# Expert stage of a hybrid layer: four couples of experts instead of two take their tokens straight from memory, empty slots are left out, and the sorted rows are fetched and transposed among the first couples' products

## The chip, the cores and the metric

The program runs on one core of a Trainium2 chip. A core has TensorE (PE) for matrix products, VectorE (DVE), ScalarE (ACT) and GpSimd (POOL) for elementwise work, SyncE (SP), from which the kernel's ordinary DMAs are issued, and 16 DMA engines that move data between memory (DRAM) and the core's SBUF. Products land in PSUM, eight banks of 128x512 float32. The metric is the device time of one execution in microseconds, as the median of three runs.

## The reference

Two layers over 512 tokens of width 1024: the first has attention, pooling and a gated MLP, the second neighbourhood attention, a gated delta rule and a hierarchical mixture of experts. The change lies in the mixture alone:

```python
N_EXPERTS, TOP_K_IN_GROUP, D_EXPERT = 64, 2, 256
def hierarchical_moe(h, wg_r, bg_r, we_r, be_r, w_gate, w_up, w_down):
    ...  # group by argmax, two experts in the group by top_k, softmax gates
    def expert_block(args):
        tok, e = args
        xb = h_pad[tok]
        hid = jax.nn.silu(xb @ w_gate[e]) * (xb @ w_up[e])
        return hid @ w_down[e]
    ...  # each row times its gate, added to its token
...
x = x + hierarchical_moe(rms_norm(x, ln2_g), ...)
```

All 64 experts' weights are read, 3 MB of float32 each; 1024 rows (512 tokens, two experts each) go through them.

## The kernel before

**Slots and couples.** Each expert has 64 slots (`CAP`). Experts e and e + 32 make a couple, whose 128 slots are the 128 rows of one tile; the 32 couples are run in order (`pr_`). A loop for experts with more than 64 rows follows, which these inputs never enter.

**One couple.** `gate_up` multiplies the transposed tokens `xw` (128 features x 8 x 128 slots) by the gate and up weights `wgu` of both experts into one bank, `pgu`, 32 products; ScalarE makes `sg` and VectorE `hid` from it. `turn` transposes `hid` into `phT`, which ScalarE evicts. `down` multiplies by `wd` into two banks, `pd`, and both halves are scaled by the gates and split into a coarse and a fine part, `og` (ScalarE, then VectorE). `combine` multiplies `og` by `OT`, which has a one where a slot belongs to a token, and so adds the rows to their tokens: the left 512 columns (n = 0) into four banks kept over all couples, `pkept`; the right 512 (n = 1) into passing banks, `pcmb`, which VectorE adds to `xn`. The order of TensorE's instructions is that of the code (a manual schedule): gate-up of couple p, down of p - 1, turn of p, combine of p - 1. The other engines' orders are set by the scheduler.

**Banks.** The eight banks go by tags, each tag's in turn: `banks = dict(mm=2, pa=2, pb=2, pc=1, gv=1)`. `pa` holds `pgu` and `phT`, `pb` holds `pd` and `pcmb`; from the first combine on `mm`, `gv` and `pc` are the four `pkept`.

**Weights.** For each couple SP issues four transfers `wgu` (10 buffers) and two `wd` (4 buffers) in one queue, each when the buffer before it is free.

**Tokens.** `xn`, the layer's input to the experts, is written to DRAM as `xs`. Couples 0 and 1 take their tokens directly: `first_i` holds each slot's token (0 for an empty slot), an indirect DMA from GpSimd's queue fetches 128 rows into `xg`, and `gather` transposes them in eight 128x128 pieces into two `pb` banks (`pxg`), each evicted by one VectorE instruction that multiplies by the norm's gain. For all later couples the 1024 rows are sorted by expert: `ptok` and vector work ahead of it give `tok_of`, `compact` fetches and transposes eight blocks of 128 sorted rows into `xgT`, and `window` copies the 64 columns of each expert from there into `xw` on GpSimd. Blocks 0 to 3 stand behind gate-up 0 and blocks 4 to 7 behind gate-up 1:

```python
                hid = gate_up(pr_)
                if first and pr_ < 2:
                    compact(4 * pr_, 4 * pr_ + 4)
```

`pgt` is the table of gates by slot (`gt`).

Of the kernel before, what the change touches and what calls it, by code (L numbers as in the profile page):

```python
# [19 lines left out]
S = 512  # L20
# [69 lines left out]
def hybrid_kernel(ctx, tc, A, out, dbg=None):  # L90
# [1205 lines left out]
    xn = [lp.tile([128, D], F32, name=f"xn{t}") for t in range(4)]  # L1296
    NPAIR = 32
# [52 lines left out]
    for c in range(4):  # L1350
        hi, lo = split_w(A["wout2"][c])
        cs = slice(c * 256, c * 256 + 256)
        for t in range(4):
# [6 lines left out]
            nc.vector.scalar_tensor_tensor(xn[t][:, cs], p[:, 256:512], ra[:, t:t + 1],  # L1360
                                           xin[2 * t + c // 2][:, c % 2 * 256:c % 2 * 256 + 256], op0=ALU.mult, op1=ALU.add)
            nc.vector.tensor_tensor(xn[t][:, cs], xn[t][:, cs], p[:, 0:256], op=ALU.add)
            nc.scalar.activation(jk, xn[t][:, cs], AF.Square, accum_out=sq3[:, t, c:c + 1])
            if c % 2:
                nc.sync.dma_start(xs[ts, c * 256 - 256:c * 256 + 256], xn[t][:, c * 256 - 256:c * 256 + 256])
# [19 lines left out]
        for k in (2 * c, 2 * c + 1):  # L1385
            pt = ps("pb", "xnT")
            for t in range(4):
                nc.tensor.transpose(pt[:, t * 128:t * 128 + 128], xn[t][:, k * 128:k * 128 + 128], ident)
# [98 lines left out]
    def gather(tok, dst, xg):  # L1487

        nc.gpsimd.indirect_dma_start(out=xg, out_offset=None, in_=xs,
                                     in_offset=bass.IndirectOffsetOnAxis(ap=tok, axis=0))  # L1490
        for q in range(2):
            p = ps("pb", "pxg")
            for j in range(4):
                nc.tensor.transpose(p[:, j * 128:j * 128 + 128], xg[:, (4 * q + j) * 128:(4 * q + j) * 128 + 128], ident)
            nc.vector.tensor_tensor(dst[:, 4 * q:4 * q + 4, :], p.rearrange("p (j s) -> p j s", j=4),
                                    V("ln2", 4 * q, 4).unsqueeze(2).to_broadcast([128, 4, 128]), op=ALU.mult)


    t2, t2r = mt("t2", (128, 8, 2)), mt("t2r", (128, 8, 2), F32R)
    one_hot(t2, e31)  # L1500
    nc.vector.tensor_tensor(t2r, t2, pay[:, :, :, 0].rearrange("p t k -> p (t k)").unsqueeze(2).to_broadcast([128, 8, 2]),
                            op=ALU.mult)
    ohs = slots("a")
    pf = ps("pc", "pfirst")
    for i in range(8):
        nc.tensor.matmul(pf[:, 0:2], ohs[:, i, :], t2r[:, i, :], start=(i == 0), stop=(i == 7))
    first_i = mt("first_i", (128, 2), I32)
    nc.vector.tensor_copy(first_i, pf[:, 0:2])
    first = []

    def direct(i):
        first.append(et("xw", (128, 8, 128)))
        gather(first_i[:, i:i + 1], first[i], et("xg", (128, D)))

    direct(0)
    direct(1)


    few = et("few", (128, 256), tag="hid")
    ge, tokb, cend = cut(few, 0, 4, 2, 9), cut(few, 72, 4, 2, 8), cut(few, 136, 64)  # L1520
    tokr, cnt, cst_ = mt("tokr", (128, 4, 2, 8), F32R), mt("cnt", (128, 64)), mt("cst_", (128, 64))
    nc.vector.tensor_copy(cnt, pk[:, 0:64])
    nc.vector.tensor_tensor_scan(cend, cnt, iota[:, 0:1].to_broadcast([128, 64]), 0.0, op0=ALU.add, op1=ALU.add)
    nc.vector.tensor_tensor(cst_, cend, cnt, op=ALU.subtract)
    place, base = m4("place", 2), m4("base", 2)
    nc.vector.tensor_tensor(scr, M, cst_.unsqueeze(1).to_broadcast([128, 8, 64]), op=ALU.mult)
    nc.vector.tensor_reduce(base, scr, axis=AX.X, op=ALU.add)
    nc.vector.tensor_tensor(place, base, rank, op=ALU.add)

    nb, sp = m4("nb", 2), m4("sp", 2)  # L1530
    nc.vector.tensor_tensor(ge, place.unsqueeze(3).to_broadcast([128, 4, 2, 9]),
                            edges.unsqueeze(1).unsqueeze(1).to_broadcast([128, 4, 2, 9]), op=ALU.is_gt)
    nc.vector.tensor_reduce(nb, ge[:, :, :, 1:8], axis=AX.X, op=ALU.add)
    nc.vector.scalar_tensor_tensor(sp, nb, -128.0, place, op0=ALU.mult, op1=ALU.add)
    nc.vector.tensor_tensor(tokb, ge[:, :, :, 0:8], ge[:, :, :, 1:9], op=ALU.subtract)
    nc.vector.tensor_tensor(tokr, tokb, pay[:, :, :, 0:1].to_broadcast([128, 4, 2, 8]), op=ALU.mult)
    pi = ps("pc", "ptok")
    for i in range(2):
        o = et("ohp", (128, 4, 128), F32R, tag="OT")
        one_hot(o, sp[:, 2 * i:2 * i + 2, :])  # L1540
        for j in range(4 * i, 4 * i + 4):
            nc.tensor.matmul(pi[:, 0:8], o[:, j % 4, :], tokr[:, j // 2, j % 2, :], start=(j == 0), stop=(j == 7))
    tok_of = mt("tok_of", (128, 8), I32)
    nc.vector.tensor_copy(tok_of, pi[:, 0:8])
# [37 lines left out]
    def compact(b0, b1):  # L1582
        for b in range(b0, b1):
            gather(tok_of[:, b:b + 1], xgT[:, :, b * 128:b * 128 + 128],
                   et("xg", (128, D)) if b // 2 % 2 else big("xg"))
# [6 lines left out]
    def moe_round(pre, wts, gt, first=()):  # L1592
# [58 lines left out]
        def combine(OT, ab, start=False, stop=False):  # L1651
# [3 lines left out]
            for n, t in ((0, 0), (0, 1), (1, 0), (0, 2), (1, 1), (0, 3), (1, 2), (1, 3)):  # L1655
# [13 lines left out]
        with tc.manual_schedule(engines={mybir.EngineType.PE}):  # L1669
            prev = None  # L1670
            for pr_ in range(NPAIR):
# [4 lines left out]
                if first and pr_ < 2:  # L1676
                    compact(4 * pr_, 4 * pr_ + 4)
# [122 lines left out]
```

## Time and profile before

| | us |
|---|---|
| median of three runs | 1586.71 (1580.32 to 1591.32) |
| the profiled execution's own time | 1585.05 |
| its span on the core | 1583.3 |
| TensorE busy in the span | 1484.3 (94%) |
| VectorE, ScalarE, GpSimd busy | 843.9, 503.3, 247.0 |

The rows of the trace come from the profiled execution, so a sum over them stands against 1585.05 and its span of 1583.3. A stretch such as 1065:1070 counts microseconds from the span's start; the expert stage begins near 1050 and ends with the span. PEclk is the TensorE clock that was granted, 1.00 for 2.4 GHz and 0.50 for 1.2 GHz. A busy share is a mean over stages that differ, so the stage is read by itself.

### The profile page before, as it was taken

How to read it: one execution, taken by the hardware profiler on the slowest of the kernel's cores; microseconds unless marked ns; L12 is line 12 of the kernel's file. 1: busy time of each engine (PE TensorE's matmuls, PEld its weight loads, DVE VectorE, ACT ScalarE, POOL GpSimd, SP SyncE). 2: the span in 40 equal slices, each digit the busy share in tenths (PEclk: the TensorE clock that was granted, in tenths of full speed). 3: DMA queues.
4: the chain of work that ended last, by engine and by line, in shares of the span. 5: the costliest groups of instructions: out<-in, count | busy, mean ns of one | idle time of the engine just before them, and what ended most of it. 6: DMA issues, size and time to landing. Idle time of an engine off the chain costs nothing.

```text
span 1583.3 us, 20312 instructions
## 1 busy us (share of the span) xinstructions
PE 1484.3 (94%) x7485; PEld 1006.7 (64%) x7485; DVE 843.9 (53%) x1673; ACT 503.3 (32%) x933; POOL 247.0 (16%) x314
## 2 busy tenths in 40 slices
PE   6989999999999999998879999968999999999997
PEld 2756686888888887876667787964444434444443
DVE  3669777563564457275796666554323323333334
ACT  3444434441342345263434435320111111111111
POOL 0233011000000005224551330101100000000000
PEclk8979999999999999998989999988999999999999
DMA  8664242322233223363332123658899999999983
GB/s 302 225 212 130 68 146 89 111 94 93 95 103 96 93 80 101 98 190 95 86 103 64 44 81 101 240 224 333 325 412 421 421 420 420 420 421 421 420 363 109
DMA packets 81741, 327.22 MB, mean 207 GB/s; under 512 B 17624, under 2 KB 21336, under 8 KB 57312
## 3 DMA queue, kind: packets, MB, share of 16 engines
q1 hardware_dynamic: 80192, 320.58, 54.6%
q0 software_dynamic: 1440, 5.24, 1.0%
q8 instruction: 61, 1.00, 0.3%
q14 instruction: 48, 0.39, 0.1%
HBM read 317.32 MB, written 8.47 MB: 206 GB/s over the span
## 4 chain that ended last, share of the span: by engine, by line
PE 71%; DVE 11%; DMA 6%; ACT 4%; POOL 3%; issue 3%; SPq 1%; POOLq 0%; ACTq 0%; DVEq 0%
PE pgu L1612 13%; PE pj L177 10%; PE pj L179 10%; PE pj L178 10%; PE pd L1641 7%; PE pcmb L1660 2%; DVE wlo L171 2%; DMA graw<-in_modw_dram 2%; PE pcmb L1659 2%; DVE og L198 2%; DMA xg<-xs,tok_of 1%; ACT og L194 1%; DVE cv L872 1%; PE pS L482 1%; PE pkept L1659 1%
## 5 line engine op out<-in xcount | busy, mean ns | idle before, releaser
L177 PE MATMUL pj<-hh,whi 128*128 128x512 f32 x640 | 260.0, 407 | 19.3 <-ACT cn L866 8.1
L179 PE MATMUL pj<-hh,wlo 128*128 128x512 f32 x640 | 257.4, 403 | 2.4 <-DVE wlo L171 2.4
L178 PE MATMUL pj<-hl,whi 128*128 128x512 f32 x640 | 257.9, 403 | 0.6 <-DVE hl L200 0.6
L1612 PE MATMUL pgu<-wgu,xw 128*64 128x512 f32 x1024 | 226.8, 595 | 0.0
L171 DVE TENSOR_TENSOR wlo<-wraw,whi 128x1024 fp32r<-128x1024 f32 (+4 forms) x126 | 151.5, 1205 | 51.0 <-ACT whi L170 47.9
L170 ACT ACTIVATE whi<-wraw 128x1024 fp32r<-128x1024 f32 (+4 forms) x126 | 129.1, 1027 | 136.9 <-PE pj L178 116.6
L1612 PEld LDWEIGHTS pgu<-wgu,xw 128*64 128x64 f32 x1024 | 70.7, 137 | 139.2 <-issue 138.8
L177 PEld LDWEIGHTS pj<-hh,whi 128*128 128x128 f32 x640 | 124.0, 194 | 53.7 <-ACT cn L866 10.6
L179 PEld LDWEIGHTS pj<-hh,wlo 128*128 128x128 f32 x640 | 124.1, 194 | 32.7 <-issue 4.4
L178 PEld LDWEIGHTS pj<-hl,whi 128*128 128x128 f32 x640 | 123.7, 193 | 28.0 <-issue 2.1
L1618 DVE SCALAR_TENSOR_TENSOR hid<-pgu,agt,sg 128x256 f32<-128x256 f32 x32 | 15.5, 483 | 200.8 <-ACT sg L1616 200.8
L1616 ACT ACTIVATE sg<-pgu,agt 128x256 f32<-128x256 f32 x32 | 15.2, 475 | 330.2 <-PE pgu L1612 330.2
L1641 PE MATMUL pd<-wd,hT 128*64 128x512 f32 x512 | 116.0, 595 | 0.2 <-issue 0.2
L1663 DVE TENSOR_TENSOR xn<-xn,pcmb 128x512 f32<-128x512 f32 x128 | 85.1, 685 | 33.7 <-PE pcmb L1660 33.7
L1603 POOL COPY xw<-xgT 128x512 f32 x60 | 35.1, 614 | 404.5 <-PE pgu L1612 386.2
L304 POOL TENSOR_TENSOR acc<-acc,sq 128x512 f32<-128x512 f32 x21 | 33.7, 1623 | 392.8 <-ACT sq L303 392.6
L198 DVE SCALAR_TENSOR_TENSOR og<-pd,agt,og 128x512 fp32r<-128x512 f32 x64 | 48.0, 750 | 78.3 <-ACT og L194 78.3
L1641 PEld LDWEIGHTS pd<-wd,hT 128*64 128x64 f32 x512 | 37.1, 138 | 73.1 <-issue 64.5
L194 ACT ACTIVATE og<-pd,agt 128x512 fp32r<-128x512 f32 x64 | 44.0, 688 | 89.5 <-PE pd L1641 89.5
L179 PE MATMUL pj<-ah,wlo 128*128 128x512 f32 x176 | 69.3, 394 | 0.0
L177 PE MATMUL pj<-ah,whi 128*128 128x512 f32 x176 | 69.3, 394 | 0.0
L178 PE MATMUL pj<-al,whi 128*128 128x512 f32 x176 | 69.3, 394 | 0.0
(445 smaller groups left out, 2602.9 us busy)
## 6 DMA issues: line engine op xcount, KB each, us to landing
wgu<-in_egu_dram SPq DMA_DIRECT2D x128, 1024.0 KB
wd<-in_ed_dram SPq DMA_DIRECT2D x62, 1024.0 KB
graw<-in_modw_dram SPq DMA_DIRECT2D x48, 512.0 KB
wraw<-in_wup_dram SPq DMA_DIRECT2D x42, 512.0 KB
wraw<-in_win_dram SPq DMA_DIRECT2D x38, 512.0 KB
wraw<-in_wdn_dram SPq DMA_DIRECT2D x20, 512.0 KB
wraw<-in_wout_dram SPq DMA_DIRECT2D x16, 512.0 KB
E<-gscr SPq DMA_DIRECT2D x16, 256.0 KB
```

Source lines behind the costliest of these rows:

```text
L170: nc.scalar.activation(hi, raw, AF.Copy)
L171: nc.vector.tensor_tensor(lo, raw, hi.bitcast(F32), op=ALU.subtract)
L177: nc.tensor.matmul(p, whi, hh, start=first, stop=False)
L178: nc.tensor.matmul(p, whi, hl, start=False, stop=False)
L179: nc.tensor.matmul(p, wlo, hh, start=False, stop=last)
L194: nc.scalar.activation(hi, src, AF.Identity, scale=scale, bias=0.0 if bias is None else bias)
L198: nc.vector.scalar_tensor_tensor(lo, src, scale, hi.bitcast(F32), op0=ALU.mult, op1=ALU.subtract)
L1603: nc.gpsimd.tensor_copy(xw[:, :, 64 * i:64 * i + 64], xgT[:, :, bass.ds(r, 64)])
L1612: nc.tensor.matmul(gu[64 * i:64 * i + 64, :], xw[:, j, 64 * i:64 * i + 64], wts.gu[e][j], start=(j == 0), stop=(j == 7))
L1641: nc.tensor.matmul(pd[64 * i:64 * i + 64, :], hT[:, j, 64 * i:64 * i + 64], wts.d[e][:, j, n * 512:n * 512 + 512], start=(j == 0), stop=(j ...
L1659: nc.tensor.matmul(pc, OT[:, ts], a, start=(n == 1 or start), stop=False, skip_group_check=(n == 0))
L1663: nc.vector.tensor_tensor(v, v, pc, op=ALU.add)
```

## The change

Four couples (`NFIRST`) take their tokens directly. An empty slot's index is now 1024, beyond the bound of 511, so that its row is not fetched; the two `xg` buffers are set to zero ahead (GpSimd). The list of the sorted rows (`sorted_tokens`, with `ptok`) stands behind gate-up 0, and so do the transposes of couples 2 and 3. The eight sorted blocks are transposed behind gate-up 1 (0, 1), combine 0 (2), gate-up 2 (3, 4), combine 1 (5) and gate-up 3 (6, 7), in `pa` and `pb`; block b + 2 is fetched when block b has been transposed. Of each pair of evictions one stays on VectorE, the other is four 128x128 instructions on ScalarE. `xn` is split: its left halves, `xl`, give their buffers to the `xw` of couples 2 and 3 and are loaded again from `xs` for the last combine; the right halves are `xr`. In `combine` the third `pkept` comes before the first `pcmb`, and the third `pcmb` uses `pa`. In the code after, `raw` are the rows fetched for the first couples, and `between` is called at the places named.

```diff
+    xl = [lp.tile([128, 2, S], F32, tag="xl", name="xl", bufs=2) for i in range(2)]
+    xr = [lp.tile([128, S], F32, name=f"xr{t}") for t in range(4)]
+    xn = [(xl[t // 2][:, t % 2, :], xr[t]) for t in range(4)]
+    NPAIR, NFIRST = 32, 4
...
-    def gather(tok, dst, xg):
+    def fetch(tok, xg, **kw):
 
         nc.gpsimd.indirect_dma_start(out=xg, out_offset=None, in_=xs,
-                                     in_offset=bass.IndirectOffsetOnAxis(ap=tok, axis=0))
+                                     in_offset=bass.IndirectOffsetOnAxis(ap=tok, axis=0), **kw)
+        return xg
+
+    def features(xg, dst, tags=("pb", "pb")):
+
         for q in range(2):
-            p = ps("pb", "pxg")
+            p = ps(tags[q], "pxg")
             for j in range(4):
                 nc.tensor.transpose(p[:, j * 128:j * 128 + 128], xg[:, (4 * q + j) * 128:(4 * q + j) * 128 + 128], ident)
-            nc.vector.tensor_tensor(dst[:, 4 * q:4 * q + 4, :], p.rearrange("p (j s) -> p j s", j=4),
-                                    V("ln2", 4 * q, 4).unsqueeze(2).to_broadcast([128, 4, 128]), op=ALU.mult)
...
+            if q == 0:
+                nc.vector.tensor_tensor(dst[:, 0:4, :], p.rearrange("p (j s) -> p j s", j=4),
+                                        V("ln2", 0, 4).unsqueeze(2).to_broadcast([128, 4, 128]), op=ALU.mult)
+            else:
+                for j in range(4):
+                    nc.scalar.activation(dst[:, 4 + j, :], p[:, j * 128:j * 128 + 128], AF.Copy, scale=V("ln2", 4 + j))
...
+    def fetch_first(i):
+        xg = et("xg", (128, D))
+        if i < 2:
+            nc.gpsimd.memset(xg, 0.0)
+        return fetch(first_i[:, i:i + 1], xg, bounds_check=S - 1, oob_is_err=False)
...
+    def fetch_block(b):
+        blocks[b] = fetch(tok_of[:, b:b + 1], big("xg") if b < 2 else et("xg", (128, D)))
+
+    def block_features(b):
+        features(blocks[b], xgT[:, :, b * 128:b * 128 + 128], ("pa", "pb") if b % 2 == 0 else ("pb", "pa"))
+        if 2 <= b + 2 < 8 and b >= 2:
+            fetch_block(b + 2)
...
+        if at == "start":
+            features(raw[0], first[0])
+            raw.append(fetch_first(2))
+            features(raw[1], first[1])
+            raw.append(fetch_first(3))
+        elif at == ("up", 0):
+            sorted_tokens()
+            fetch_block(0)
+            fetch_block(1)
+            for i in (2, 3):
+                first.append(new_first(i))
+                features(raw[i], first[i], ("pa", "pb"))
+                fetch_block(i)
+        elif at == "last":
+
+            for i in range(2):
+                xl[i] = lt("xl", (128, 2, S), tag="xl", bufs=2)
+                nc.sync.dma_start(xl[i], xs[256 * i:256 * i + 256, 0:S].rearrange("(t p) c -> p t c", t=2))
...
+        for b in {("up", 1): (0, 1), ("add", 0): (2,), ("up", 2): (3, 4), ("add", 1): (5,), ("up", 3): (6, 7)}.get(at, ()):
+            block_features(b)
...
-            for n, t in ((0, 0), (0, 1), (1, 0), (0, 2), (1, 1), (0, 3), (1, 2), (1, 3)):
+            for n, t in ((0, 0), (0, 1), (0, 2), (1, 0), (0, 3), (1, 1), (1, 2), (1, 3)):
                 a, b = ab[n]
                 ts = slice(t * 128, t * 128 + 128)
-                pc = ps("pb", "pcmb") if n else kept[t]
+                pc = ps("pa" if t == 2 else "pb", "pcmb") if n else kept[t]
```

On TensorE, between the last product of gate-up 0 and the first of gate-up 1, there stood before (four blocks of the sorted rows, then the turn of couple 0):

```order
L1612 MATMUL pgu_9309<-wgu_8744,xw_9191 64x512
L1494 MATMUL pxg_9332<-cst_64,xg_9330 128x128 x4
L1494 MATMUL pxg_9338<-cst_64,xg_9330 128x128 x4
...
L1494 MATMUL pxg_9374<-cst_64,xg_9372 128x128 x4
L1494 MATMUL pxg_9380<-cst_64,xg_9372 128x128 x4
L1626 MATMUL phT_9386<-cst_64,hid_9328 128x128 x2
L1612 MATMUL pgu_9405<-wgu_9076,xw_9206 64x512
```

and stands now:

```order
L1662 MATMUL pgu_9317<-wgu_8746,xw_9261 64x512
L1592 MATMUL ptok_9338<-tokr_9242,ohp_9339 128x8 x4
L1592 MATMUL ptok_9338<-tokr_9242,ohp_9345 128x8 x4
L1501 MATMUL pxg_9357<-cst_64,xg_9286 128x128 x4
L1501 MATMUL pxg_9363<-cst_64,xg_9286 128x128 x4
L1501 MATMUL pxg_9375<-cst_64,xg_9305 128x128 x4
L1501 MATMUL pxg_9381<-cst_64,xg_9305 128x128 x4
L1676 MATMUL phT_9392<-cst_64,hid_9336 128x128 x2
L1662 MATMUL pgu_9411<-wgu_9078,xw_9262 64x512
```

The four sorted blocks have left this place; `ptok` and the transposes of couples 2 and 3 have come.

On TensorE, in the combine of couple 0 behind the turn of couple 1, there stood before (`pkept_9505` to `_9508` are the four kept banks):

```order
L1659 MATMUL pkept_9506<-og_9487,OT_9391 128x512
L1660 MATMUL pkept_9506<-og_9487,OT_9391 128x512
L1659 MATMUL pcmb_9513<-og_9495,OT_9391 128x512
L1660 MATMUL pcmb_9513<-og_9495,OT_9391 128x512
L1659 MATMUL pkept_9507<-og_9487,OT_9391 128x512
L1660 MATMUL pkept_9507<-og_9487,OT_9391 128x512
```

and stands now (`pkept_9485` to `_9488`):

```order
L1709 MATMUL pkept_9486<-og_9467,OT_9397 128x512
L1710 MATMUL pkept_9486<-og_9467,OT_9397 128x512
L1709 MATMUL pkept_9487<-og_9467,OT_9397 128x512
L1710 MATMUL pkept_9487<-og_9467,OT_9397 128x512
L1709 MATMUL pcmb_9495<-og_9475,OT_9397 128x512
L1710 MATMUL pcmb_9495<-og_9475,OT_9397 128x512
L1709 MATMUL pkept_9488<-og_9467,OT_9397 128x512
```

A third kept pair has come ahead of the first passing one, in every couple.

On GpSimd, whose queue holds the gathers, there stood before (the last six of ten gathers are left out):

```order
L1416 MEMSET xgT_9093 128x8x64
L1489 DMA xg_9192<-xs_8464,first_i_9189 128x1024
L1489 DMA xg_9207<-xs_8464,first_i_9189 128x1024
L1489 DMA xg_9358<-xs_8464,tok_of_9253 128x1024
L1489 DMA xg_9372<-xs_8464,tok_of_9253 128x1024
```

and stand now:

```order
L1524 MEMSET xg_9193 128x1024
L1524 MEMSET xg_9198 128x1024
L1492 DMA xg_9193<-xs_8466,first_i_9191 128x1024
L1492 DMA xg_9198<-xs_8466,first_i_9191 128x1024
L1492 DMA xg_9286<-xs_8466,first_i_9191 128x1024
L1492 DMA xg_9305<-xs_8466,first_i_9191 128x1024
L1492 DMA xg_9352<-xs_8466,tok_of_9260 128x1024
```

Two memsets have come ahead, and there are twelve gathers instead of ten.

## Rows read from the trace of the kernel before

**Rows 1.** Table by stretches: each engine's busy us, PEclk, DMA share, GB/s.

```profile
core 0: us, PE busy (x) PEld busy (x) DVE busy (x) ACT busy (x) POOL busy (x), PEclk, DMA share, GB/s
1065.00:1070.00 5.00, 1.87 (x8) 1.78 (x8) 4.05 (x19) 0.00 (x0) 2.16 (x2) 0.50 0.49 146
1100.00:1105.00 5.00, 1.84 (x8) 1.47 (x8) 1.59 (x3) 0.00 (x0) 0.00 (x0) 0.71 1.02 423
1120.00:1125.00 5.00, 5.00 (x26) 1.68 (x24) 0.48 (x1) 0.48 (x1) 1.17 (x2) 1.00 0.76 269
1125.00:1130.00 5.00, 4.95 (x23) 2.66 (x20) 2.19 (x3) 1.65 (x3) 0.00 (x0) 1.00 1.02 428
1200.00:1300.00 100.00, 99.60 (x442) 42.46 (x440) 34.80 (x55) 14.39 (x27) 7.03 (x12) 1.00 1.01 420
```

**Rows 2.** Chain of work that ended last: start us, us, what.

```profile
1065.14 5.54 DMA xg<-xs,first_i
...
1089.32 16.31 DMA xg<-xs,tok_of
...
1146.53 7.02 PE pgu L1612 x32
1153.55 3.48 PE pd L1641 x16
...
1551.51 7.02 PE pgu L1612 x32
```

**Rows 3.** Order of time ahead of gate-up 0: start, us, instruction, [idle before it <-releaser].

```profile
1065.14 1.21 POOL L1489 DMA_INDIRECT xg<-xs,first_i  x1 [11.38 <-DVE first_i L1508]
...
1067.58 1.87 PE L1542 MATMUL ptok<-tokr,ohp 128*128 128x8 f32 x8 [2.94 <-DVE ohp L1470]
...
1070.72 1.97 PE L1494 MATMUL pxg<-cst,xg 128*128 128x128 f32 x8 [1.27 <-DMA xg<-xs,first_i]
...
1074.13 1.38 PE L1494 MATMUL pxg<-cst,xg 128*128 128x128 f32 x8
...
1076.31 1.94 PE L1612 MATMUL pgu<-wgu,xw 128*64 128x512 f32 x8
```

**Rows 4.** The tile `xg`: the gathers' time from issue to landing.

```profile
DMA to landing us min/median/max: 4.3/5.9/16.3
```

**Rows 5.** Groups of instructions by form: count, busy us, mean ns, idle before.

```profile
L1495 DVE TENSOR_TENSOR xgT<-pxg,vec 128x512 f32<-128x512 f32 x16 | 10.5, 685 | 12.6 <-PE pxg L1494 12.6
...
L510 ACT ACTIVATE PT<-pT 128x128 f32<-128x128 f32 x32 | 8.0, 270 | 10.7 <-DVE PT L512 10.7
```

**Rows 6.** Order of time: two gathers issued, and the transposes behind their landing.

```profile
1086.30 0.94 POOL L1489 DMA_INDIRECT xg<-xs,tok_of  x1 [0.66 <-PE pxg L1494]
...
1087.88 0.94 POOL L1489 DMA_INDIRECT xg<-xs,tok_of  x1 [0.65 <-PE pxg L1494]
...
1098.26 1.06 PE L1494 MATMUL pxg<-cst,xg 128*128 128x128 f32 x8 [0.95 <-DMA xg<-xs,tok_of]
1102.01 1.84 PE L1494 MATMUL pxg<-cst,xg 128*128 128x128 f32 x8 [2.69 <-DMA xg<-xs,tok_of]
```

**Rows 7.** Order of time on TensorE, part of a combine (couple 1).

```profile
1128.15 0.40 PE L1659 MATMUL pcmb<-og,OT 128*128 128x512 f32 x1
1128.59 0.50 PE L1660 MATMUL pcmb<-og,OT 128*128 128x512 f32 x1
1128.93 0.39 PE L1659 MATMUL pkept<-og,OT 128*128 128x512 f32 x1
1129.16 0.40 PE L1660 MATMUL pkept<-og,OT 128*128 128x512 f32 x1
...
1130.80 0.50 PE L1659 MATMUL pcmb<-og,OT 128*128 128x512 f32 x1
1131.14 0.39 PE L1660 MATMUL pcmb<-og,OT 128*128 128x512 f32 x1
```

**Rows 8.** The page's DMA issues: count, KB each.

```profile
wgu<-in_egu_dram SPq DMA_DIRECT2D x128, 1024.0 KB
```

**Rows 9.** Two of SP's issues of weights beside couple 2, in order of time.

```profile
1120.15 4.24 SPq L1311 DMA_DIRECT2D wgu<-in_egu_dram  x4
1127.02 0.80 SPq L1321 DMA_DIRECT2D wd<-in_ed_dram  x2
```

## What the change should do to the time

> **What bounds the kernel.** I read the table by stretches first, then the chain of waits, the order of time around the change, and the DMA views. From the expert stage on TensorE is busy 99.6% of the time with the clock granted in full, while the weights stream at 420 GB/s and the 16 DMA engines are busy throughout [rows 1]. Which of the two sets the pace? The chain of waits has no weight transfer in it: it runs through TensorE, and each couple of experts takes the same time, (1551.51 - 1146.53) / 27 = 15.00 us [rows 2]. So TensorE's own order is the bound there, with the weights close behind. Ahead of it lies a stretch of waiting: the first couple's gather is 5.54 us of the chain, a later one 16.31 us, TensorE is busy 1.84 us in the five from 1100, and the granted clock falls to 0.50 (1.2 GHz) from 1065 and to 0.71 in the mean at 1100 [rows 1, 2]. The first gate-up product starts at 1076.31 [rows 3]; the fifth (couple 4) at 1146.53, 70.2 us later [rows 2]. The change touches the start, these 70.2 us, and one thing in every later couple: the order of the adds.
>
> **The start.** Up to the first gather nothing on the path changes: `first_i` is computed for four couples instead of two in instructions of a few columns. The two memsets stand ahead of it on GpSimd, which was idle for 11.38 us there [rows 3], so they cost nothing; if that cover were gone they would delay the gather by their own length, two instructions of 128x1024. The first gather is issued at 1065.14 and takes 5.54 us [rows 2] for 128 rows, of which those of the empty slots are all token 0. An expert has on average 512 x 2 / 64 = 16 tokens for 64 slots, so about a quarter of the rows is left. No row shows a gather of a quarter. The quickest whole one takes 4.3 us [rows 4]; the bounds are 5.5 (nothing gained) and, since some data must still come, 3.3; I take 4.3, because that is a measured gather without repeated rows. Landing: 1069.4. The Trainium skill (DMA: Bandwidth & Descriptors, "Anatomy of one DMA - SWDGE (gpsimd) path") gives about 2.0 us and the bytes at 436 GB/s, which is 3.2 us for 128 rows, where the trace has 4.3 at best, and 2.3 us for a quarter; by it the start would come 2.0 us earlier than I take and the sum below would be 1567.
>
> The sorted rows' list, 1.87 us of `ptok` at half clock and the vector work behind it, leaves this stretch, and the gate table `pgt` moves into the wait for the gather, where it is hidden. After landing: eight transposes of couple 0, 1.97 us in the order of time before; couple 1's second bank then waits until ScalarE has emptied couple 0's second one in four pieces. A 128x128 eviction on ScalarE is 270 ns [rows 5], so 1.1 us against 0.69 us for VectorE's one instruction; then four transposes at half clock, 0.9 us (half of the 1.97, or 1.38 for eight across a clock change [rows 3]). 1069.4 + 2.0 + 1.1 + 0.9 = 1073.4 instead of 1076.31: **2.9 us** gained, 1.6 with the slow landing, 3.9 with the quick one.
>
> **Couples 0 to 3.** TensorE's work from the first gate-up to that of couple 4, at the new pace of a couple (14.57 us, next part): three whole couples 43.7, gate-up and turn of the fourth 7.4, the 64 transposes of the sorted rows 8 x 1.06 = 8.5 [rows 6], those of couples 2 and 3 2.1, `ptok` 0.9 at full clock. Sum 62.6. New is one wait for a bank: `pa` has two, and couple 3's first transposes need the one that gate-up 0 fills, so they wait for `sg` and `hid` behind it, some 1.3 us with the vector work queued ahead; 63.9. Then the gathers. Four in a row beside the weights landed 3.75 us apart (1098.26, 1102.01), and the second had been issued 11.96 us before [rows 6], so a single one takes about 11.96 - 3.75 + 1.6 (their distance at issue) = 9.8 us. Now they are issued far ahead: blocks 0 and 1 about 8.5 us after the first gate-up starts, needed at 18.6; block 4 is issued when block 2 is transposed, at 30, and needed at 38. That is 1 to 2 us late in two or three places. I take 3 us, between 0 and 6. 63.9 + 3 = 66.9 against 70.2: **3.3 us** gained, between 0.3 and 6.3. ScalarE gets eight half blocks of 1.1 us in a stretch where it is nearly idle, and the evictions of `pd` stand behind two of them; TensorE needs longer for the transposes and `pd` itself than ScalarE for these, so I cost that at nothing. If that cover fails, a couple costs 1 us more.
>
> **Every couple: the order of the adds.** Matmuls of this part normally start 0.23 us apart (1128.93 to 1129.16). The one at 1128.59 starts 0.44 us after its forerunner, waiting for VectorE's second half of `og`, and the restart costs 0.34 instead of 0.23 to the next; at 1130.80 the last `pcmb` waits for a bank that VectorE has to empty, and its restart is 0.34 again [rows 7]. Excess: 0.21 + 0.11 + 0.11 = 0.43 us in 15.00. Now a third `pkept` pair stands ahead, 0.47 us, which is more than the 0.21 of waiting; and the third `pcmb` goes to `pa`, so the last one needs a bank that was read one add earlier. `pa` is free then: its other users, the gate-up and `phT`, have been read. So 15.00 becomes 14.57. Late next would be the weights. Couples 4 to 31 give 27 x 0.43 = 11.6, the last combine in the loop 0.4: **12.0 us**. The tail behind it (eight adds on VectorE and the outputs) keeps its length; the reload of `xl` is 1 MB (2.5 us at 420 GB/s) in the middle of the weights' queue.
>
> **Do the weights keep up?** A couple needs 6 transfers of 1024 KB [rows 8], 6.29 MB; in 14.57 us that is 432 GB/s, and the best stretch shows 428, the steady one 420 [rows 1]. At 420 a couple's weights take 15.0 us, so they fall behind by 0.43 us a couple, 11.6 us in all, plus 2.5 for the reload: 14.1. The lead: `wd` issued at 1127.02 is used from 1153.55 [rows 2, 9]; the couple's transfers begin at 1120.15 [rows 9], with the engines not full before (0.76 [rows 1]), so they have landed by 1120.2 + 15.0 = 1135.2. Lead 18 us. It holds, with 4 us left. The Trainium skill speaks against this: by DMA: Bandwidth & Descriptors, "Where 436 GB/s comes from", the HBM side of about 358 GB/s binds such loads, which would be 17.6 us a couple; the trace's 420 over 100 us says otherwise. HBM Reference, "Specifications", has about 425 for a core that streams alone, near what the rows show.
>
> **Sum.** 2.9 + 3.3 + 12.0 = 18.2 us. The profiled execution takes 1585.05, so 1566.9; it lies 1.7 under the median of 1586.71, and from the median it is 1568.5. I forecast **1569 us**.
>
> **Rivals.** (1) The weights bind: their rate falls under the 420, or the lead is shorter than I think, and couples return to 15.0 us. For it: 432 GB/s is more than any row shows. Against it: TensorE never waited for them. If from the first couple on, only the first two terms stay, 6.2: 1581; if half way, 1575. 17%. (2) The first couples wait as before for gathers and banks: the gain is 12.0 and the start, less some 6 us: 1578. For it: gathers beside weights took up to 16.3 us [rows 4], and ScalarE has new work. 13%. (3) Slower: every gather takes the 16.31 us of [rows 2], not 9.8. Blocks 0 and 1 then come 8 us late, block 4 8, block 7 8, and three pauses drop the clock, at about 2 us each: 30 us of loss instead of 3, so 27 - 18.2 = 9 us slower, 1596. It decides from 21 us of added waits. Against it: the 16.31 was the fourth of four in one queue, now they go by ones and twos. 5%. (4) Better: no gather is late and the first is quick, 1563 to 1565. 8%. The forecast, 1563 to 1574, has 57%.
>
> The range of 1562 to 1581 leaves out the slower rival and the ends. A change of under 1% (15.9 us) can hardly be told from none here; the runs before are 11 us apart. Below 1570.8 lie four fifths of the forecast's share, the better case and little of the first rival: 55% faster; 41% within 1%; 4% slower.
>
> **What would show it.** Right: gate-up 0 near 1073.4, gate-up of couple 4 about 67 us later, then 14.57 us a couple with `pcmb` no longer waiting for `og`; no pause over 3 us in between. Wrong: a wait of gate-up or `pd` for `wgu` or `wd` late in the stage (rival 1), waits of `pxg` for `xg` with a granted clock of 0.50 (rivals 2 and 3), or couples still at 15.00 without any wait for weights, which would mean that I misread what the adds cost.

## The result and the profile after

The changed kernel takes 1563.84 us in the median of four runs (1561.53 to 1565.13), the kernel before 1586.03 in four (1580.32 to 1591.32); the ratio is 0.9859, with a 95% interval of 0.9823 to 0.9896. 1569 was forecast, with a range of 1562 to 1581. The profiled execution took 1565.13, its span is 1563.3.

Where did the 19.9 us between the two profiled executions (1585.05 and 1565.13) come from? The order of time gives the starts of the same instructions in both traces: the last transpose `xnT` of the stage ahead of the experts, gate-up 0, the gate-ups of couples 4 and 31, and the end.

| stretch | before | after | gained | forecast |
|---|---|---|---|---|
| start of the span to the last `xnT` | 1050.20 | 1051.19 | -0.99 | 0 |
| to gate-up 0 | 26.11 | 22.96 | 3.15 | 2.9 |
| to gate-up of couple 4 | 70.15 | 65.09 | 5.06 | 3.3 |
| to gate-up of couple 31 | 404.98 | 392.94 | 12.04 | 11.6 |
| to the end | 31.81 | 31.16 | 0.65 | 0.4 |

The first line has nothing to do with the change: in the 14 profiles of this study the last `xnT` starts between 1045.0 and 1051.2, whichever kernel it is, and in two of the changed kernel at 1051.2 and 1047.6. It is the reason to compare kernels stretch by stretch below, not by single times.

The table by stretches, for the changed kernel (columns as in [rows 1]):

```profile
1065.00:1070.00 5.00, 4.14 (x20) 4.06 (x20) 2.89 (x12) 0.00 (x0) 2.25 (x2) 0.50 0.24 83
1070.00:1075.00 5.00, 3.95 (x23) 2.80 (x24) 3.73 (x13) 1.89 (x7) 1.50 (x2) 0.85 0.21 53
...
1090.00:1095.00 5.00, 4.86 (x30) 2.49 (x28) 1.77 (x3) 2.36 (x9) 0.00 (x0) 1.00 1.02 416
...
1100.00:1105.00 5.00, 5.00 (x27) 3.03 (x27) 3.56 (x6) 1.14 (x4) 0.94 (x1) 1.00 1.02 424
...
1200.00:1300.00 100.00, 100.00 (x456) 44.64 (x454) 33.89 (x55) 14.85 (x28) 8.26 (x14) 1.00 1.01 421
```

TensorE, busy 1.84 us of the five from 1100 at a clock of 0.71 before [rows 1], is busy throughout at 1.00, and in the hundred from 1200 its 99.60 have become 100.00. The DMA engines are as full as before. The clock also comes back earlier at the start: the five from 1070 have 0.85 in the mean, and had 0.52 before:

```profile
1070.00:1075.00 5.00, 4.28 (x21) 4.28 (x22) 1.83 (x6) 0.00 (x0) 0.94 (x1) 0.52 0.30 84
```

The chain that ended last (start us, us, what):

```profile
1074.22 7.02 PE pgu L1662 x32
...
1111.26 8.74 DMA xg<-xs,tok_of
...
1121.78 8.63 DMA xg<-xs,tok_of
...
1139.31 7.02 PE pgu L1662 x32
...
1532.25 7.02 PE pgu L1662 x32
```

The 16.31 us of a gather [rows 2] are gone from it; two of 8.7 remain. From couple 4 on, (1532.25 - 1139.31) / 27 = 14.55 us a couple.

TensorE in the same place of a combine as [rows 7] (couple 1):

```profile
1117.83 0.40 PE L1710 MATMUL pkept<-og,OT 128*128 128x512 f32 x1
1118.07 0.39 PE L1709 MATMUL pcmb<-og,OT 128*128 128x512 f32 x1
1118.30 0.39 PE L1710 MATMUL pcmb<-og,OT 128*128 128x512 f32 x1
1118.53 0.40 PE L1709 MATMUL pkept<-og,OT 128*128 128x512 f32 x1
...
1119.70 0.39 PE L1710 MATMUL pcmb<-og,OT 128*128 128x512 f32 x1
1119.93 0.40 PE L1709 MATMUL pcmb<-og,OT 128*128 128x512 f32 x1
1120.17 0.39 PE L1710 MATMUL pcmb<-og,OT 128*128 128x512 f32 x1
```

Every start is 0.23 us behind the last, at `og` and at the last `pcmb` too: no wait and no restart is left.

The start, in order of time (the columns of [rows 3]):

```profile
1066.04 0.16 DVE L1519 TENSOR_SCALAR first_i<-pfirst 128x4 int32<-128x4 f32 x1 [0.95 <-PE pfirst L1517]
...
1066.86 3.73 PE L1557 MATMUL pgt<-table,ohs 128*128 128x96 f32 x16 [0.86 <-DVE table L1553]
1067.09 1.26 POOL L1492 DMA_INDIRECT xg<-xs,first_i  x1 [10.56 <-issue]
...
1070.60 1.48 PE L1501 MATMUL pxg<-cst,xg 128*128 128x128 f32 x8
1071.78 0.68 DVE L1473 TENSOR_TENSOR ohp<-iota,sp 128x512 fp32r<-128x512 f32 x1
...
1073.12 1.09 PE L1501 MATMUL pxg<-cst,xg 128*128 128x128 f32 x8 [1.04 <-DVE xw L1503]
1074.15 7.09 PE L1662 MATMUL pgu<-wgu,xw 128*64 128x512 f32 x32
```

The gather is issued 0.89 us behind the end of `first_i` (1066.20), where it had been 0.30; the gate table, 3.73 us at half clock, ends at 1070.59, and the transposes follow at once, so no wait for the gather shows (it lands at nearly the same moment: in e12_changed_again, the same kernel, 4.37 us behind `first_i`, and the table ends at 4.38); `ohp`, part of the sorted list, holds VectorE from 1071.78 when the first bank is ready to be emptied, and couple 1's transposes wait 1.04 us for it.

The tile `xg`:

```profile
DMA to landing us min/median/max: 3.2/8.6/15.1
```

A gather with a quarter of the rows takes 3.2 us at the least, where a whole one took 4.3 [rows 4]. A late one still takes 15.1, but its rows aren't needed by then. TensorE's waits from 1060 to 1142 (us in total, times, longest):

```profile
PE pxg L1501 <- DMA xg<-xs,tok_of: 1.8, 2, 1.0
...
PE pxg L1501 <- DVE xw L1503: 1.4, 2, 1.0
```

Behind gate-up 0 that is 1.8 for gathers and 0.35 for a bank.

### The profile page after: what moved, and what is told of

Read it like the earlier page. It is cut to its first block, busy times and chain, and to the rows that moved or that the text cites. A ratio compares the mean times of both kernels' runs of the same rounds, so it can differ in the third digit from the quotient of the medians.

```text
span 1563.3 us, 20383 instructions
## 1 busy us (share of the span) xinstructions
PE 1472.4 (94%) x7501; PEld 1009.8 (65%) x7501; DVE 835.6 (53%) x1665; ACT 516.3 (33%) x981; POOL 248.3 (16%) x314
## 4 chain that ended last, share of the span: by engine, by line
PE 75%; DVE 9%; DMA 6%; POOL 3%; issue 3%; ACT 3%; SPq 1%; DVEq 0%; POOLq 0%; ACTq 0%
PE pgu L1662 14%; PE pj L177 10%; PE pj L179 10%; PE pj L178 10%; PE pd L1691 7%; DMA graw<-in_modw_dram 3%; PE pkept L1709 2%; PE pkept L1710 2%; PE pcmb L1709 2%; PE pcmb L1710 2%; DVE wlo L171 1%; DVE cv L872 1%; DMA xg<-xs,tok_of 1%; PE pS L482 1%; PE po L178 1%
## 5 line engine op out<-in xcount | busy, mean ns | idle before, releaser
L1713 DVE TENSOR_TENSOR xr<-xr,pcmb 128x512 f32<-128x512 f32 x128 | 82.2, 683 | 30.3 <-PE pcmb L1710 30.3
```

The source lines that it names most:

```text
L1713: nc.vector.tensor_tensor(v, v, pc, op=ALU.add)
```

## The experiments

The stretches of all kernels, from the starts in the order of time (`first_i`: its end); "a couple" is the steady distance of gate-ups. Spans and times are named where they count.

| kernel | `xnT` to `first_i` | to gate-up 0 | gate-up 0 to 4 | a couple |
|---|---|---|---|---|
| before | 14.64 | 11.47 | 70.15 | 15.00 |
| changed | 15.02 | 7.94 | 65.09 | 14.55 |
| e1_new_adds_alone | 14.63 | 11.48 | 69.22 | 14.56 |
| e2_order_alone | 14.64 | 11.31 | 72.18 | 15.14 |
| e3_bank_alone | 14.64 | 10.95 | 69.87 | 14.88 |
| e4_old_adds | 15.02 | 8.82 | 67.23 | 15.00 |
| e5_all_slots | 14.65 | 9.65 | 68.61 | 14.55 |
| e6_blocks_in_fours | 15.01 | 8.17 | 81.37 | 14.55 |
| e7_vector_evicts | 15.02 | 8.11 | 65.32 | 14.55 |
| e8_extra_transfers | 15.03 | 8.82 | 65.90 | 14.55 |
| e9_two_mends | 14.65 | 7.98 | 64.95 | 14.55 |
| e10_extra_behind_rows | 15.03 | 8.82 | 65.79 | 14.55, then 14.91 |
| e11_all_slots_again | 14.65 | 10.10 | 71.66 | 14.55 |
| e12_changed_again | 15.02 | 7.94 | 65.29 | 14.55 |

One difference in the second and third columns is the clock's and not a kernel's. Eight of these traces have the changed start with its unfetched slots. In five of them (the changed kernel, e6, e7, e9, e12) the granted clock is back at 1.00 5.2 to 6.1 us behind `first_i`; in e4_old_adds, e8_extra_transfers and e10_extra_behind_rows, whose code is the changed kernel's up to there, TensorE has done the same work until then, and the clock stays at 0.50 until 10.0 to 10.4 us. There gate-up 0 comes at 8.82 instead of 7.94 to 8.17, and gate-up 1 takes another 0.4 to 0.8 us longer to follow: some 1.5 us in the two columns.

**e1_new_adds_alone**, the kernel before with two lines of the change:

```diff
-            for n, t in ((0, 0), (0, 1), (1, 0), (0, 2), (1, 1), (0, 3), (1, 2), (1, 3)):
+            for n, t in ((0, 0), (0, 1), (0, 2), (1, 0), (0, 3), (1, 1), (1, 2), (1, 3)):
-                pc = ps("pb", "pcmb") if n else kept[t]
+                pc = ps("pa" if t == 2 else "pb", "pcmb") if n else kept[t]
```

> The kernel before with nothing but the new order of the adds and the third passing product in pa. Theory A (the steady gain is the order of the adds and its bank, and nothing else): a couple takes 14.55 us instead of 15.00, as in the changed kernel; the stretch up to the first gate-up and the 70.2 us of the first four couples stay as before, less 0.4 us for each of the combines in them; 12 to 13 us less than before, about 1573. Rival B (the pace came with the rest of the change, the split of xn or the work given to ScalarE): couples stay at 15.00 and the time at 1586.

Measured: 1565.96 us, ratio to before 0.9902 (0.9863 to 0.9941). Gate-up 4 to 31 takes 393.12 instead of 404.98, 11.9 us less, and the early couples 0.9 less; the start is as before. The steady gain is those two lines, and nothing else of the change. In the median this kernel is 16.3 us below the kernel before (1582.22 beside it), more than the 12.8 us of these stretches; its last `xnT`, ahead of the change, comes at 1045.03, the earliest of all profiles.

**e2_order_alone** has the first of the two, **e3_bank_alone** the second.

> The kernel before with the new order of the adds, all passing products in pb. Theory A (order and bank belong together): the wait for og goes, but the last passing product now comes 0.47 us earlier to a bank that VectorE empties no earlier than before, at 0.6 us for each add: 14.8 to 15.05 us a couple. Rival B (the order alone does it): 14.55.

> The kernel before with the third passing product in pa, the old order of the adds. Theory A: only the restart at the last passing product goes, 0.12 us; the wait for og and its restart, 0.32, stay: 14.88 us a couple. Rival B (the bank alone does it): 14.55. Rival C (the wait for og was hidden anyway): 15.00.

Measured: 15.14 and 14.88 us a couple (times of 1590.9 and 1578.39, one each). The bank alone is worth 0.12, as expected to the hundredth. The order alone makes a couple 0.14 longer than before, a little beyond the range expected. TensorE in e2_order_alone, end of a combine:

```profile
1298.34 0.40 PE L1660 MATMUL pcmb<-og,OT 128*128 128x512 f32 x1
1298.58 0.50 PE L1659 MATMUL pcmb<-og,OT 128*128 128x512 f32 x1
1298.92 0.40 PE L1660 MATMUL pcmb<-og,OT 128*128 128x512 f32 x1
1299.51 0.50 PE L1659 MATMUL pcmb<-og,OT 128*128 128x512 f32 x1 [0.20 <-DVE xn L1663]
1299.85 0.40 PE L1660 MATMUL pcmb<-og,OT 128*128 128x512 f32 x1
1300.18 0.65 PE L1612 MATMUL pgu<-wgu,xw 128*64 128x512 f32 x2
```

Two products now wait for a bank: after 1298.58 the next start is 0.34 away, after 1298.92 it is 0.59, after 1299.51 0.34, where 0.23 is usual: 0.11 + 0.36 + 0.11 = 0.58 us, more than the 0.43 that the old order lost. The third bank is what lets the order pay.

**e4_old_adds** is the other way round: the changed kernel with those two lines as before.

> The changed kernel with the old order of the adds and all passing products in pb: the first two terms alone. Theory A (the terms add up): couples at 15.00, gate-up 0 where the changed kernel has it (1074.2), couple 4 about 66.5 us later (0.45 more in each of three combines), 12 to 13 us more than the changed kernel, 1576 to 1577, and 9 to 10 us less than before. Rival B (the early couples' gain hangs on the new adds): under 5 us less than before, 1581 or more.

Measured: 1577.6 us, ratio to before 0.9958 (0.9939 to 0.9977); gate-up 0 at 1074.06, 67.23 us for the early couples, 15.00 a couple. The time alone doesn't decide: 1577.6 is close to theory A's 1576 to 1577, but it is only 4.6 us below the kernel before (1582.22), which is rival B's "under 5" and not A's 9 to 10. The stretches tell them apart. The first two terms gain 2.3 and 2.9 us here, in a trace where the clock comes back late; beside e8 and e10, where it does so too and the new adds are in place, the early couples are 1.3 to 1.4 us longer, which is three combines at 0.45. So the terms add up, as theory A has it; its 9 to 10 us were reckoned from a trace where the clock comes back early, and from a kernel before of 1586.03. The two ratios multiply to 0.9902 x 0.9958 = 0.9860 where the whole has 0.9859; with intervals of 0.4% and 0.2% to either side, so close a match is chance.

**e5_all_slots** and, the same kernel, **e11_all_slots_again** fetch the empty slots:

```diff
-    nc.vector.scalar_tensor_tensor(t2r, pay[:, :, :, 0].rearrange("p t k -> p (t k)").unsqueeze(2).to_broadcast([128, 8, NFIRST]),
-                                   -1024.0, t2, op0=ALU.add, op1=ALU.mult)
+    nc.vector.tensor_tensor(t2r, t2, pay[:, :, :, 0].rearrange("p t k -> p (t k)").unsqueeze(2).to_broadcast([128, 8, NFIRST]),
+                            op=ALU.mult)
...
-    nc.vector.tensor_scalar(first_i, pf[:, 0:NFIRST], 1024.0, None, op0=ALU.add)
+    nc.vector.tensor_copy(first_i, pf[:, 0:NFIRST])
...
-        if i < 2:
-            nc.gpsimd.memset(xg, 0.0)
-        return fetch(first_i[:, i:i + 1], xg, bounds_check=S - 1, oob_is_err=False)
+        return fetch(first_i[:, i:i + 1], xg)
```

> The changed kernel with the empty slots fetched (index 0, no bound, no memsets). Theory A (unfetched slots shorten the start): the first gather takes 5.5 us again instead of 3.2, is issued 0.3 us behind first_i instead of 0.9, and VectorE is spared the 0.4 us that the two memsets cost it; from the end of first_i to gate-up 0 it takes 8.6 to 9.4 us instead of 7.94, and couples 0 to 3 stay at 65 us. Rival B (the gate table's 3.7 us on TensorE and the bound's own cost hide the shorter gather): 7.9 us or less.

> The kernel with the empty slots fetched once more, since its longer couples (68.6 us against 65.1) rest on one wait of 2.5 us for a block of sorted rows in one trace. Theory A (the unfetched slots shorten both stretches): 9.4 to 9.9 us from first_i to gate-up 0 and over 67 us from there to couple 4. Rival B (the wait for the block came by chance): 65 to 66 us.

Measured: from `first_i` to gate-up 0 9.65 and 10.10 us, against 7.94 to 8.82 in the kernels that leave the empty slots out, both a little beyond the ranges expected; and 68.6 and 71.7 us for the early couples, against 65 to 66. The second was not foreseen. In both traces the clock is back at 1.00 only 10.7 to 10.8 us behind `first_i`, so the like cases are e4, e8 and e10: against their 8.82 the whole gathers cost 0.8 and 1.3 us at the start, and whether they also hold the clock down two traces can't tell. The wait view of e11 (1060 to 1150):

```profile
PE pxg L1501 <- DMA xg<-xs,tok_of: 4.9, 2, 2.6
PE pxg L1501 <- DMA xg<-xs,first_i: 1.4, 1, 1.4
```

and what the first of the two long waits does, by stretches:

```profile
1090.00:1095.00 5.00, 2.39 (x14) 1.90 (x12) 1.70 (x3) 1.14 (x4) 0.00 (x0) 0.73 1.02 423
1095.00:1100.00 5.00, 5.00 (x15) 1.53 (x16) 0.45 (x2) 1.83 (x5) 0.00 (x0) 0.59 1.02 416
```

Sorted block 1 is waited for, 2.5 us in e5 and 2.6 in e11, and behind that pause the granted clock falls to 0.66 and 0.59 in the mean of the next five us: `pd` takes 5.62 us there instead of the 3.65 of the changed kernel. A pause of 2.6 us costs some 4.6. Why does block 1, issued 10 to 11 us behind the start of gate-up 0 in all four, land 19 us behind it in the changed kernel and 22 when the gathers ahead of it are whole? These have ended by then, but the DMA packets show a part of the answer. In the changed kernel the four `wgu` issued in the first 8 us behind that start have moved by 17 us, the next two have hardly begun, and around this gap the gathers move 75 and 101 rows in one us each, where beside the weights they move some 35. With whole gathers these weights begin later and more slowly, behind the last rows for couple 3; they are through 1 to 2 us later, and the best us of the gathers has 82 rows (e5) and 54 (e11). That this gap is the whole of the 3 us isn't shown.

**e6_blocks_in_fours** puts the eight blocks back into two groups, with four direct couples:

```diff
-        for b in {("up", 1): (0, 1), ("add", 0): (2,), ("up", 2): (3, 4), ("add", 1): (5,), ("up", 3): (6, 7)}.get(at, ()):
+        for b in {("up", 1): (0, 1, 2, 3), ("up", 2): (4, 5, 6, 7)}.get(at, ()):
```

> The changed kernel with blocks 0 to 3 all behind gate-up 1 and 4 to 7 all behind gate-up 2. Theory A (the early couples' gain is that gathers are out long before their rows are needed): blocks 2 and 3 are waited for, to 15 us after their issue, some 8 us; blocks 6 and 7, fetched only when 4 and 5 have been transposed, 8.6 us each with one overlapping the other, some 9 us; the 65.1 us from gate-up 0 to that of couple 4 become 79 to 84. Rival B (the gain is four direct couples, wherever the blocks stand): 65 to 68.

Measured: 81.37 us, in the range of theory A, and longer than before the change. Its chain and waits, then the stretches of the second pause:

```profile
1098.09 8.25 DMA xg<-xs,tok_of
1119.17 8.75 DMA xg<-xs,tok_of
```

```profile
PE pxg L1501 <- DMA xg<-xs,tok_of: 13.3, 4, 8.3
```

```profile
1120.00:1125.00 5.00, 0.00 (x0) 0.00 (x0) 0.13 (x1) 1.11 (x5) 1.04 (x2) 0.68 1.00 423
1125.00:1130.00 5.00, 1.95 (x10) 1.98 (x11) 0.69 (x1) 0.00 (x0) 0.00 (x0) 0.50 0.72 295
```

13.3 us of waits instead of 1.8, with the clock down behind each: where the blocks stand is worth 16 us here. Not all of it is the place itself: a block is still fetched only when the one two ahead of it has been transposed, so that in the second group blocks 6 and 7 are also fetched late (the 8.3 us are the wait for block 6), and this run doesn't part the two. Four direct couples with the blocks so placed and fetched are slower than the kernel before (70.15).

**e7_vector_evicts** empties every transposed bank on VectorE:

```diff
-            if q == 0:
-                nc.vector.tensor_tensor(dst[:, 0:4, :], p.rearrange("p (j s) -> p j s", j=4),
-                                        V("ln2", 0, 4).unsqueeze(2).to_broadcast([128, 4, 128]), op=ALU.mult)
-            else:
-                for j in range(4):
-                    nc.scalar.activation(dst[:, 4 + j, :], p[:, j * 128:j * 128 + 128], AF.Copy, scale=V("ln2", 4 + j))
+            nc.vector.tensor_tensor(dst[:, 4 * q:4 * q + 4, :], p.rearrange("p (j s) -> p j s", j=4),
+                                    V("ln2", 4 * q, 4).unsqueeze(2).to_broadcast([128, 4, 128]), op=ALU.mult)
```

> The changed kernel with every eviction of a transposed bank on VectorE, none on ScalarE. Theory A (who evicts is off the path): 65.1 us from gate-up 0 to that of couple 4, within 0.7; the start within 0.5. Rival B (without ScalarE, VectorE's 0.69 us for each of eight blocks and two couples is waited for): 68 us or more.

Measured: 65.32 and 8.11 us, and one time of 1563.43. Theory A: ScalarE's part in the evictions is worth nothing that shows.

**e8_extra_transfers** was to test how near the weights are:

```diff
+                if between is at_place and pr_ in (12, 14, 16, 18):
+                    spare = drp.tile([128, 4, 512], F32, name=f"spare{pr_}")
+                    nc.sync.dma_start(spare, A["egu"][pr_][:, 0:4, :])
```

> The changed kernel with four more transfers of 1 MB (weights copied from memory to memory) in the weights' queue, ahead of couples 12, 14, 16 and 18. The least time from a landing of wd to its use was 5.0 us, in the last couples, falling by 0.42 us a couple. Theory A (the weights are behind TensorE by this margin): at 2.5 us each they shift all later landings by 10 us, so that pd waits in the last couples and the stage ends 5 us later; 20 us of shift and 15 us later if a copy holds the engines twice. Rival B (the queue has rate to spare and catches up): no wait, couples at 14.55 to the end.

It says nothing on that. The copies depend on nothing, and the scheduler had placed them far ahead: SP issued the first at 48.66 us and the last at 117. **e10_extra_behind_rows** copies sorted rows instead, which exist only from couple 3 on:

```diff
+                if pre == "a" and pr_ in (12, 14, 16, 18):
+                    spare = drp.tile([128, 2, 1024], F32, name=f"spare{pr_}")
+                    nc.sync.dma_start(spare, xgT[:, pr_ // 2 - 6:pr_ // 2 - 4, 0:2 * S])
```

> The changed kernel with four more transfers of 1 MB in the weights' queue ahead of couples 12, 14, 16 and 18, this time of the sorted rows from SBUF to memory, so that they can't be issued before these rows are there (the copies of weights had been issued in the stage ahead of the experts). Theory A as there: the least time from a landing of wd to its use is 5.0 us, the four shift later landings by 10 us, pd waits from about couple 18 on, and the stage ends 5 us later (15 if a transfer holds the engines twice). Rival B: the queue has rate to spare, no wait, couples at 14.55 to the end.

Here a landing was taken as the time when as many 8 KB packets had ended as were queued up to it. Measured: gate-up 4 to 31 takes 401.43 us instead of 392.94, 8.5 more and not 5. The first longer couple is the one of gate-up 18 (14.78); the waits of `pd` for `wd` are plain in the couple of gate-up 20, which takes 17.38:

```profile
1376.67 1.04 PE L1691 MATMUL pd<-wd,hT 128*64 128x512 f32 x2 [0.22 <-DMA wd<-in_ed_dram]
1379.07 3.65 PE L1691 MATMUL pd<-wd,hT 128*64 128x512 f32 x14 [1.35 <-DMA wd<-in_ed_dram]
```

```profile
1420.00:1520.00 100.00, 99.16 (x438) 46.10 (x435) 31.70 (x51) 14.87 (x28) 8.22 (x14) 1.00 1.01 421
```

Behind it a couple takes 14.91 us, which is 6.29 MB / 14.91 us = 422 GB/s, the rate of the row: that is the weights' own pace (one couple, of gate-up 23, takes 16.45). The extra 4.19 MB at 421 GB/s are 10.0 us, of which 8.5 show, so this run had 1.5 us to spare and not 5.0. The trace also records when each of the 16 parts of a transfer ends, and TensorE waits for the last: in e10 `pd` goes on 0.04 us behind it in nearly every couple from 17 on. By the last part, the least time from a landing of `wd` to its use is 3.3 us in the changed kernel and 3.2 in e12_changed_again (couple 29, falling by 0.36 us a couple); the count of packets takes it as landed 1.7 to 1.8 us too early there. In e10 it is 3.4 us too early in the last couples: one transfer lands 4.03 us behind the one ahead of it, where 2.48 is usual, and the later ones stay late by as much, which is the couple of 16.45. Such late landings are in every trace, by chance as far as the runs show: over the eight kernels whose couples take 14.55 us to the end, the margin lies between 0.9 (e8_extra_transfers) and 3.3.

**e9_two_mends** takes up two costs seen in the profile after, the memsets on GpSimd and the list's work on VectorE:

```diff
-            nc.gpsimd.memset(xg, 0.0)
+            for h in range(2):
+                nc.scalar.activation(xg[:, S * h:S * h + S], iota, AF.Copy, scale=0.0)
...
     def sorted_tokens():
+        nc.vector.tensor_tensor(scr, M, cst_.unsqueeze(1).to_broadcast([128, 8, 64]), op=ALU.mult)
+        nc.vector.tensor_reduce(base, scr, axis=AX.X, op=ALU.add)
...
+        nc.vector.tensor_tensor(tokr, tokb, pay[:, :, :, 0:1].to_broadcast([128, 4, 2, 8]), op=ALU.mult)
```

> The changed kernel with the two memsets turned into four ScalarE instructions and the vector work for the sorted list (from place to tokr) written behind gate-up 0. Theory A (the memsets slow VectorE by 0.37 us, and the list's second-last instruction on VectorE delays the first eviction by some 0.5 to 0.9): from the last xnT to the end of first_i 14.65 us instead of 15.02, from there to gate-up 0 7.0 to 8.0 instead of 7.94 to 8.82, couples 0 to 3 as before within 1 us; about 1 us less in all, too little for the times. Rival B (the first gather and the gate table are what ends last): from first_i to gate-up 0 unchanged.

Measured: 14.65 us to `first_i`, as expected, and 7.98 to gate-up 0, no less than the changed kernel's, which rival B had too. The second mend did not take place: VectorE's order is the scheduler's, which set `ohp` ahead of the first eviction again, so its cost was not tried. The time, 1562.56 (1561.5 to 1563.42), ratio to before 0.9885 (0.9864 to 0.9905), can't be told from that of the changed kernel. **e12_changed_again** is the changed kernel once more, for the spread.

> The changed kernel once more, for the spread of its stretches: 7.9 to 8.8 us from first_i to gate-up 0, 65 to 66 us from there to couple 4, 14.55 us a couple; waits for a block of sorted rows of at most 2 us in sum.

Measured: 15.02 us to `first_i`, then 7.94, 65.29 and 14.55 us as expected, waits for blocks of 2.2 us in sum, a little over the 2.

## Why the prediction was right, point by point

**Every couple.** 0.43 us of excess was read from the starts of one combine, and the couples became 0.45 shorter, 15.00 to 14.55; e1_new_adds_alone and e4_old_adds show that the order and its bank do it, e2_order_alone and e3_bank_alone that they do it only together. This term carried the forecast, and it was right because each part of it was a distance between two starts in the trace.

**The start.** 2.9 us were forecast and 3.15 came, by a different sum, so the match is luck. The gather was taken at 4.3 us; it takes 3.4 to 3.6 in the traces that have its landing, and the quick bound of 3.3, for which the text had no row, is near what came. Against that stand two costs that the sum did not have: the bound delays the issue (0.89 us behind `first_i` instead of 0.30; 0.88 in e9_two_mends, which has the bound and no memsets), and the memsets, costed at nothing because GpSimd was idle, lengthen the way to `first_i` by 0.37 us (15.02 against 14.64; 14.65 without them in e5_all_slots, e9_two_mends and e11_all_slots_again). And `pgt`, said to be hidden in the wait for the gather, is as long as this wait: it ends at 1070.59, and the next gain there needs both shorter. The sum also had the transposes at half clock throughout; that the clock came back in the middle of them is a gain it did not foresee, and not a steady one: in the three traces where it comes back late the gain up to gate-up 0 is 2.3 us, and in e8 and e10 the gain of the early couples is 4.3, 6.6 us together beside the 6.2 forecast and the 8.2 of the changed kernel's trace.

**Couples 0 to 3.** 3.3 us were forecast, 5.06 came: the mis-sized terms are the waits. The bank was to cost 1.3 us and costs 0.35, by the wait view for the eviction of couple 2's bank and not for `hid`, and the gathers were to cost 3 us and cost 1.8. A single gather beside the weights takes 8.6 to 8.7 us where 9.8 was worked out. What the prediction missed is on what this gain hangs: with whole gathers (e5_all_slots, e11_all_slots_again) it is 1.5 us gained or 1.5 lost, 68.6 and 71.7 against 70.15. The unfetched slots were costed for the first gather alone.

**The rivals.** The first (the weights bind) did not come. Its margin, "4 us left", is 3.3 in the changed kernel's trace, close to the text, but by errors that cancel. The lead at the beginning was counted too long: 18 us, where the last part of that couple's second `wd` lands 14.5 us ahead of its use; the text took the weights as landed when the queue's bytes had passed. The reload of `xl`, to which the text gave 2.5 us in the middle of the weights' queue, is issued at 1530.87, behind the last weights, and costs nothing. And the lead shrinks by 0.43 us a couple in the mean from couple 4 to 29, as worked out, but as 0.36 and a few late landings. That the margin can be 0.9 or 1.5 in another execution was not in the text: there the rival was much nearer. The second and third rivals (waits for gathers, with the clock) are real mechanisms that the placement avoids: e6_blocks_in_fours has them, at 16.3 us, though with later fetches as well. In the price of the third, blocks 0 and 1 are 6 us late by the text's own numbers (8.5 + 16.3 against 18.6), not 8. Their price of about 2 us for the clock behind a pause agrees with the 2.0 us by which `pd` is longer in e11.

**The sum.** 18.2 us were forecast on the span, 19.9 measured, of which the stage ahead, not touched by the change, took 1.0 back: the change itself is worth 20.9 in these two traces, some 1.5 of them by the clock. The medians are 22.2 apart, but the kernel before took 1579.80 in the median of seven later runs, and the changed kernel 1561.88 in one beside them: 17.9. That single microseconds of the forecast agree is therefore chance; that each of the three terms is there, and near its size, is not.

## What to carry to other kernels

Read a loop's excess from the distances between starts, and ask of each wait which engine frees the thing waited for: a new order without a bank to go with it cost 0.14 us a couple, with it gained 0.45. Issue a gather when its index is ready and place its consumer a gather's length later, among work that needs nothing of it: the same twelve gathers cost 1.8 us of waits, or 13.3 where blocks were grouped and so also fetched later, and the clock fell behind each long pause. When a loop gets faster, test what comes next by slowing that one thing by a known amount: four transfers showed that 1.5 us were left in that run, where a count of bytes had said 5. And take a landing from the last part of the transfer waited for: that gave 3.3 without an experiment, and showed that it differs from run to run.

## What the runs showed of the hardware that was not expected

A memset on GpSimd stops short VectorE instructions. The memsets and VectorE in the changed kernel, and VectorE in e9_two_mends, which has no memsets there:

```profile
1054.68 1.84 POOL L1524 MEMSET xg<- 128x1024 f32 x2
...
1055.92 0.64 DVE L1532 TENSOR_SCALAR ngm<-routing 128x4 f32<-128x4 f32 x1
1056.03 0.53 DVE L1435 CAST gif<-gix 128x4 f32<-128x4 uint32 x1
```

```profile
1054.59 0.15 DVE L1533 TENSOR_SCALAR ngm<-routing 128x4 f32<-128x4 f32 x1
1054.71 0.17 DVE L1435 CAST gif<-gix 128x4 f32<-128x4 uint32 x1
```

Both end at 1056.56, just behind the memsets (1056.52), while the instructions of other kinds ahead of them keep their length. The Trainium skill (SBUF — State Buffer, "Who interferes with whom") has the rule: the two engines share a pair of ports, which one instruction holds to its end, and casts and `tensor_scalar` are among the VectorE operations that can need it. The trace agrees, and gives the price here: 0.37 us on the path, in every one of the profiles with the memsets.

The parts of a transfer don't land together. In the changed kernel a 1 MB transfer of weights begins to land 2.9 to 3.5 us before its last part, late in the stage, and in e8_extra_transfers up to 5.9; a part that has fallen behind stays behind in all the transfers that follow it without a gap.

The weights run at 420 to 422 GB/s when nothing else limits them, in e10_extra_behind_rows with TensorE waiting for them. The HBM side of about 358 GB/s, which the Trainium skill (DMA: Bandwidth & Descriptors, "Where 436 GB/s comes from") takes as the limit, is not the one that binds this core.
